# Gates read back and multiplied block by block ahead of the second expert product, in place of all of them during the first

## The chip, the core and the metric

The kernel runs on one core of a Trainium2 chip. The core has five engines with a queue each, and each runs its queue strictly in order: PE (TensorE, matrix products, with its weight loads shown as PEld), DVE (VectorE), ACT (ScalarE), POOL (GpSimd) and SP (SyncE, which here only issues DMAs). The metric is device microseconds of one execution, as the median of several runs.

## What is computed

The reference is one block of a gated delta-rule layer followed by one block with sparse attention and a mixture of single-neuron experts. The change touches only the experts. For 256 tokens `xc`, 16 experts are picked for each of 8 heads out of 16384:

```python
gate = jax.nn.softmax(best, axis=-1)
u_sel = u[expert]
v_sel = v[expert]
act = jax.nn.gelu(jnp.einsum('td,thkd->thk', xc, u_sel), approximate=False)
return jnp.einsum('thk,thkd->td', (gate * act), v_sel)
```

The kernel gathers nothing. It computes all 16384 activations `gelu(xc @ u.T)`, multiplies them with a gate that is zero for every expert that was not picked, and multiplies the result with all of `v`.

## The kernel before

**Tiling.** The 16384 experts are 128 blocks of 128. `G` is a tile of 128 partitions (experts of a block) by 128 blocks by 256 tokens in SBUF. The first expert product (`wstat` over `w_u`) fills it: each block takes 2 granules of weights (128 x 1024 values, 512 KB), 48 matmuls of 256 columns, and a Gelu on ACT for every two blocks. The second expert product (`w_v`, the loop `for half in range(2)`) runs over the blocks again, twice, once for each half of the 2048 output columns; block i takes one granule and 12 matmuls of 512 columns, 6 for each half of the tokens.

**Splits.** Each float32 operand is split into a high and a low part, and a product is three matmuls (high x high, high x low, low x high). `Stream` does this for the weights: SP loads a granule (`wraw`), ACT copies it to `wh`, DVE subtracts to get `wl`. There are three buffers of each, so that a granule can be split when PE has released the one three before. `split_h(i)` does the same for block i of `G` (ACT, then DVE; tiles `eog`, `eghl`, `eoj`, `ewg` in turn), two blocks ahead of PE.

**Gates.** `route()` picks the experts of each head, `gates_of(h)` computes gates and addresses (DVE), and 256 indirect DMAs of POOL scatter them into two arrays in HBM, `W_d[t]` for the two halves of 128 tokens, which are zeroed earlier. When the last scatter is issued, `gating()` starts: it reads `W_d` back in 64 loads of 256 KB (4 blocks, 128 tokens each; POOL's queue; three buffers, tags `og2`, `ghl` and `wt`), and for each load DVE multiplies the 4 blocks of `G` in place (128 x 512 elements). All 64 pairs are written before `drain()` returns, that is, before the second product begins. The tags `og2` and `ghl` are also those of two of the four kinds of `split_h` tiles.

**Other work of POOL and DVE in the second product.** `residual()` loads 8 pieces of the residual and 16 rows of layer-norm parameters (256 KB each, POOL's queue) and multiplies and adds them in `res_chunk` (16 instructions of DVE on 128 x 512 elements).

**What sets the order.** The program is written out by a Python model: generators in `sides` are pumped after each few matmuls, and `clk` holds a modelled time of PE, ACT, DVE and POOL, to which each instruction adds a price (`Paced`). `after(us)`, `on(engines)` and `spare(engine, us)` let a generator wait for these clocks. The model fixes only the order of each queue; on the chip, semaphores decide. As every instruction but the weight DMAs passes through one helper, all have line 129 in the profile, and are told apart by their tiles.

Of the kernel before, what the change touches and what calls it, by code (L numbers as in the profile page):

```python
# [10 lines left out]
F32 = mybir.dt.float32  # L11
F32R = mybir.dt.float32r
BF16 = mybir.dt.bfloat16
U32 = mybir.dt.uint32
# [3 lines left out]
OP = mybir.AluOpType  # L18
# [20 lines left out]
class Stream:  # L39
# [63 lines left out]
    def next(self, ahead=True):  # L103
        if ahead:
            self.ahead()
        while self.ns <= self.ng:
            self._split()
        p = self.parts.pop(self.ng)
        self.ng += 1
        return p  # L110
# [23 lines left out]
def _free(ap):  # L134
    return int(np.prod(ap.shape[1:]))
# [24 lines left out]
def tile_blocks(ctx, tc, P, out, dbg=None, stop=None):  # L160
    nc = tc.nc
    clk = {e: 0.0 for e in "PAVG"}
# [1 line left out]
    act = Paced(nc.scalar, "A", clk, _act_price())  # L164
    dve = Paced(nc.vector, "V", clk, lambda op, kw: 0.16 + 1.04e-3 * max(
        _free(kw[n]) for n in ("out", "in_", "in_values") if n in kw))
    pool = Paced(nc.gpsimd, "G", clk, lambda op, kw: 1.0 if op == "dma_start" else 2.4 if op == "indirect_dma_start" else 0.33 + 3.2e-3 * _free(kw["out"]))
    dbg = dbg or {}

    def ident_act(out, in_, scale=1.0, bias=0.0):  # L170
# [2 lines left out]
    def copy_act(out, in_):  # L173
        act.activation(out=out, in_=in_, func=AF.Copy)

    def tt(out, a, b, op):
        dve.tensor_tensor(out=out, in0=a, in1=b, op=op)
# [25 lines left out]
    def _take(side):  # L203
        s = free.pop(0)
        t = psp.tile([128, 512], F32, name=f"bank{s}")
        held[id(t)] = (s, side, t)
        side_held[0] += side
        return t
# [14 lines left out]
    def bank():  # L223

        n = 0
        while not free:
            pump()
            n += 1
            assert n < 1000
        return _take(0)  # L230

    granules, start = [], {}
    for nm in ("w_kv", "w_dn", "w_out", "w_in2", "w_out2", "w_q", "w_u", "w_v"):
        if nm in P:
            a = P[nm]
# [30 lines left out]
    def pump(n=1):  # L266
        for _ in range(n):
            if clk["P"] == mark[0]:
                clk["P"] += 0.4
            mark[0] = clk["P"]  # L270
            for g in list(sides):
                try:
                    next(g)
                except StopIteration:
                    sides.remove(g)

    def after(us):

        t = clk["P"] + us
        while clk["P"] < t:  # L280
            yield

    def on(engines="", lat=0.3):

        t = max([clk["P"]] + [clk[e] for e in engines]) + lat
        while clk["P"] < t:
            yield

    def spare(e, us):

        while clk[e] > clk["P"] + us:
            yield
# [16 lines left out]

    def wstat(n, xh, xl, nk, done, side=1, pre=None):  # L310

        for c0 in range(0, n, 2):
            m = min(2, n - c0)
            pt = bank()
            for c in range(m):
                for g in range(nk // 8):
                    wh, wl = (t.rearrange("p (k e) -> p k e", e=128) for t in ws.next())
                    for k in range(8):
                        kk = g * 8 + k
                        if pre is not None and c0 + c == 0:  # L320
# [864 lines left out]
    W_d = [dram.tile([128, 128, 128], F32, name=f"W_d{t}") for t in range(2)]  # L1185
# [359 lines left out]
    G = gp.tile([128, 128, T], F32, name="G")  # L1545
    rs_ = ExitStack()
    ctx.callback(rs_.close)
    rp = rs_.enter_context(tc.tile_pool(name="rp", bufs=1, side="right"))
    ghl = rp.tile([128, 2, T], F32R, name="ghl")
    for tag, n in (("og2", 1), ("oj", 2), ("wg", 2)):  # L1550
        for _ in range(n):
            rp.tile([128, (2 if n == 1 else 1) * T], F32R, name="e" + tag, tag=tag, bufs=n)
    rp.tile([128, 24], F32, name="gap")
    small = rp.tile([128, 64], F32, name="small")
    wt0 = rp.tile([128, 2, 2, 128], F32, name="wt")
    put_at = wt0[:, 0].rearrange("p a t -> p (a t)").rearrange("p (t k) -> p t k", t=2).bitcast(U32)
    put_val = wt0[:, 1].rearrange("p a t -> p (a t)").rearrange("p (t k) -> p t k", t=2)

    def carve(b0, shape, dt=F32):

# [29 lines left out]
    pool.iota(tok, pattern=[[0, 1]], base=0, channel_multiplier=1, allow_small_or_imprecise_dtypes=True)  # L1590
    sk = carve(83, [2, 128])
    act.dma_start(out=sk, in_=P["sk"])
    st4 = {"q": 0, "ib": 0, "put": 0}

    def q_done(c0, m, pt):
        copy_act(qp[:, c0:c0 + 2, :], pt.rearrange("p (c t) -> p c t", c=2))
# [12 lines left out]
    def route():  # L1609
        for h in range(8):  # L1610
            while st4["q"] <= h:
                yield
            ps = yield from get()
            for t in range(2):
                for f in range(2):
                    pe.matmul(out=ps[:, (2 * t + f) * 128:(2 * t + f) * 128 + 128],
                              lhsT=qp[:, 2 * h + f, t * 128:t * 128 + 128], rhs=sk[:, f, :], start=True, stop=True)
            yield
            s = ssb[h % 2]
            copy_act(s, ps.rearrange("p (t f k) -> p t f k", t=2, f=2))  # L1620
            put(ps)
            yield from on("A")
            for t in range(2):
                for f in range(2):
                    top16(vals[:, t, h, f, :], idxs[:, t, h, f, :], s[:, t, f, :], wrk[:, :128])
                    yield from spare("V", SV)
                tt(cand, bc(vals[:, t, h, 0, :, None], [128, 16, 16]), bc(vals[:, t, h, 1, None, :], [128, 16, 16]), OP.add)
                top16(best[:, t, h, :], pos[:, t, h, :], cand.rearrange("p a b -> p (a b)"), wrk)
                yield from spare("V", SV)
            yield from gates_of(h)  # L1630
        sides.append(gating())
# [39 lines left out]
    def gating():  # L1671

        wts = []

        def load(n):
            b, t = 4 * (n // 2), n % 2
            wt = rp.tile([128, 4, 128], F32, name="wt", tag=WT[n % 3])
            pool.dma_start(out=wt, in_=W_d[t][:, b:b + 4, :])
            wts.append(wt)

        yield from on("G", 4)
        for n in range(2):
            load(n)
        yield from after(4)
        for n in range(64):
            b, t = 4 * (n // 2), n % 2
            if n + 2 < 64:
                load(n + 2)
            while st4["ib"] < b + 4:
                yield  # L1690
            g = G[:, b:b + 4, t * 128:t * 128 + 128]
            tt(g, g, wts[n], OP.mult)
            yield from after(1.0)
            yield from spare("V", 1.5)
        split_h(0)
        split_h(1)

    WT = ("og2", "ghl", "wt")
    HS = {}
    EH = (("og2", 1), ("ghl", 1), ("oj", 2), ("wg", 2))  # L1700

    def split_h(i):

        i = i % 128
        tag, n = EH[i % 4]
        if n == 1:
            e = rp.tile([128, 2, T], F32R, name="e" + tag, tag=tag)
            a, b = e[:, 0, :], e[:, 1, :]
        else:
            a, b = (rp.tile([128, T], F32R, name="e" + tag, tag=tag, bufs=2) for _ in range(2))  # L1710
        copy_act(a, G[:, i, :])
        dve.follow("A")
        tt(b, G[:, i, :], a.bitcast(F32), OP.subtract)
        HS[i] = (a, b)
# [8 lines left out]
        drain()  # L1723
        return
    wstat(128, hh, hl, KT, u_done)
    drain()
    hs.close()


    vp = ctx.enter_context(tc.tile_pool(name="vp", bufs=1))  # L1730
    hres = vp.tile([128, 2, D], F32, name="hres")
    row = [vp.tile([128, D], F32, name=f"row{n}") for n in range(2)]
    bst2 = small[:, :48].rearrange("p (m c s) -> p m c s", m=2, c=4)
    mv2 = small[:, 48:52].rearrange("p (m s) -> p m s", m=2)
    rs2, wk2, nm2 = (small[:, n:n + 2].rearrange("p (m s) -> p m s", s=1) for n in (52, 54, 56))
    dg = rp.tile([128, 2, 128], F32, name="dg", tag="wt")
    st5 = {"res": False}
    RES = 4

# [62 lines left out]
    for half in range(2):  # L1802
# [14 lines left out]
        if half == 0:  # L1817
            while not st5["res"]:
                pump()
            for m in range(2):  # L1820
                for n in range(2):
                    sides.append(later(v_sum_g, n, m, acc[m][n]))
    drain()
    fin = [[bank() for _ in range(2)] for _ in range(2)]
    for m in range(2):
        for n in range(2):
# [145 lines left out]
```

## Time and profile before

| | us |
|---|---|
| median of 3 runs | 2832.1 |
| the runs | 2824.86 to 2833.19 |
| the profiled execution | 2828.32 |
| its span, first to last instruction | 2826.6 |
| PE busy | 2743.3 (97%) |
| DVE busy | 1829.9 (65%) |
| ACT busy | 1401.8 (50%) |
| POOL busy | 630.3 (22%) |

Times within the trace count from the start of the span. The first expert product ends at 2079.5 us, the second begins at 2106.5 us, its second half at about 2454 us. The granted clock of PE is given as a share of full speed (2.4 GHz).

### The profile page before, as it was taken

Reading aid. Unit: us, or ns where it says so; the run is one execution under the profiler, and the core shown is the slowest. Engines: PE = TensorE matmul, PEld = TensorE weight load, DVE = VectorE, ACT = ScalarE, POOL = GpSimd, SP = SyncE. Lnnn points to the kernel's source line nnn. Section 1 sums busy time; section 2 is a strip of 40 time slices with the busy share of each in tenths; the row PEclk is TensorE's granted clock in tenths of the full one; section 3 lists DMA queues with packets and bytes.
Section 4 is the critical chain, followed back from the end, with each engine's and each line's share of the span. In section 5 each row is a group of like instructions: output and inputs, shape, how many; then the busy total and the mean of one; then the engine's idle time right before and its main releaser. Section 6 shows DMA issues by size and latency. Waiting matters only on the chain.

```text
span 2826.6 us, 49454 instructions
## 1 busy us (share of the span) xinstructions
PE 2743.3 (97%) x19193; PEld 2520.4 (89%) x19193; DVE 1829.9 (65%) x3447; ACT 1401.8 (50%) x1955; POOL 630.3 (22%) x917
## 2 busy tenths in 40 slices
PE   9999999999999999999999999999759999999998
PEld 7999999999788999889999999999748888888886
DVE  5747777775654746657999995444556655665555
ACT  7456666665543545444544454444225455555553
POOL 0001546654001000000444444455330000000000
PEclk9999999999999999999999999999889999999999
DMA  8536655555588885456665666666786766666664
GB/s 302 184 121 188 202 162 179 168 171 160 192 247 239 255 256 179 150 164 197 181 193 180 187 194 197 195 194 195 238 279 205 221 194 194 191 196 194 194 194 134
DMA packets 170363, 555.83 MB, mean 197 GB/s; under 512 B 29088, under 2 KB 30680, under 8 KB 169616
## 3 DMA queue, kind: packets, MB, share of 16 engines
q1 hardware_dynamic: 144720, 507.05, 57.7%
q0 software_dynamic: 21584, 36.36, 4.8%
q10 hardware_dynamic: 3824, 9.26, 0.9%
q8 instruction: 150, 2.46, 0.4%
q14 instruction: 85, 0.70, 0.1%
HBM read 529.61 MB, written 22.90 MB: 195 GB/s over the span
## 4 chain that ended last, share of the span: by engine, by line
PE 89%; DMA 5%; DVE 4%; issue 1%; ACT 1%; POOL 0%; ACTq 0%; SPq 0%; DVEq 0%; POOLq 0%
PE bank L129 89%; DMA wt<-W_d 2%; DVE wl L129 1%; DVE G L129 1%; DMA W_d<-wt 1%; DMA wrawwraw<-in_w_kv 0%; DMA wrawwraw<-in_w_out 0%; DVE hres L129 0%; ACT wh L129 0%; DMA wrawwraw<-in_w_v 0%; DVE small L129 0%; ACT y L129 0%; DMA hot<-in_bucket_hot 0%; DMA hres<-n_d 0%; DVE sso L129 0%
## 5 line engine op out<-in xcount | busy, mean ns | idle before, releaser
L129 DVE TENSOR_TENSOR wl<-wrawwraw,wh 128x1024 fp32r<-128x1024 f32 (+1 forms) x837 | 1021.8, 1224 | 748.0 <-ACT wh L129 746.8
L129 ACT ACTIVATE wh<-wrawwraw 128x1024 fp32r<-128x1024 f32 (+1 forms) x837 | 885.9, 1059 | 1106.3 <-PE bank L129 889.1
L129 PE MATMUL bank<-hh,wl 128*128 128x256 f32 x3376 | 940.6, 279 | 22.6 <-DVE wl L129 22.6
L129 PE MATMUL bank<-hh,wh 128*128 128x256 f32 x3376 | 947.1, 281 | 1.1 <-ACT hh L129 1.1
L129 PE MATMUL bank<-hl,wh 128*128 128x256 f32 x3376 | 939.3, 278 | 0.1
L129 PEld LDWEIGHTS bank<-hh,wl 128*128 128x128 f32 x3376 | 637.2, 189 | 25.7 <-DVE wl L129 25.5
L129 PEld LDWEIGHTS bank<-hh,wh 128*128 128x128 f32 x3376 | 637.5, 189 | 2.6 <-ACT hh L129 1.5
L129 PEld LDWEIGHTS bank<-hl,wh 128*128 128x128 f32 x3376 | 637.9, 189 | 0.8 <-DVE hl L129 0.5
L129 POOL DMA_INDIRECT W_d<-wt x256 | 313.6, 1225 | 392.8 <-DVE G L129 177.2
L129 PE MATMUL bank<-wh,eog 128*128 128x512 f32 x512 | 148.3, 391 | 27.0 <-ACT eog L129 27.0
L129 DVE TENSOR_TENSOR wlx<-wrawx,whx 128x1024 fp32r<-128x1024 f32 x96 | 118.0, 1230 | 82.2 <-ACT whx L129 82.1
L129 ACT ACTIVATE whx<-wrawx 128x1024 fp32r<-128x1024 f32 x96 | 101.8, 1060 | 120.8 <-PE bank L129 106.8
L129 PE MATMUL bank<-wh,ewg 128*128 128x512 f32 x512 | 147.4, 389 | 0.0
L129 PE MATMUL bank<-wh,eoj 128*128 128x512 f32 x512 | 147.4, 389 | 0.0
L129 PE MATMUL bank<-wh,eghl 128*128 128x512 f32 x512 | 147.4, 389 | 0.0
L129 PEld LDWEIGHTS bank<-wh,eog 128*128 128x128 f32 x512 | 96.7, 189 | 47.2 <-ACT eog L129 27.2
L129 POOL TENSOR_TENSOR hres<-hres,row 128x512 f32<-128x512 f32 x4 | 5.8, 1476 | 575.6 <-DVE hres L129 575.6
L129 PEld LDWEIGHTS bank<-wh,eoj 128*128 128x128 f32 x512 | 96.1, 188 | 20.0
L129 PEld LDWEIGHTS bank<-wh,eghl 128*128 128x128 f32 x512 | 96.2, 188 | 19.9
L129 PEld LDWEIGHTS bank<-wh,ewg 128*128 128x128 f32 x512 | 96.1, 188 | 20.0
L129 PE MATMUL bank<-gh,wh 128*128 128x256 f32 x392 | 110.6, 282 | 0.0
L129 PE MATMUL bank<-gl,wh 128*128 128x256 f32 x392 | 108.4, 277 | 0.0
(381 smaller groups left out, 4448.7 us busy)
## 6 DMA issues: line engine op xcount, KB each, us to landing
wrawwraw<-in_w_u SPq DMA_DIRECT2D x256, 512.0 KB, 4.2
wrawwraw<-in_w_v SPq DMA_DIRECT2D x256, 512.0 KB, 4.3
wrawwraw<-in_w_dn SPq DMA_DIRECT2D x134, 512.0 KB, 4.2
wrawwraw<-in_w_out SPq DMA_DIRECT2D x73, 512.0 KB, 3.9
wrawwraw<-in_w_in SPq DMA_DIRECT2D x61, 512.0 KB, 4.6
wrawx<-in_w_dn SPq DMA_DIRECT2D x44, 512.0 KB, 3.7
W_d<-y SPq DMA_DIRECT2D x64, 256.0 KB, 5.5
wrawwraw<-in_w_q SPq DMA_DIRECT2D x32, 512.0 KB, 3.8
```

The costliest lines, as they stand in the source:

```text
L129: return f(*a, **kw)
```

## The change

- `gating()` now goes block by block. A load is two DMAs of 64 KB (128 partitions x 128 tokens each) for the two halves of the tokens, into one of three buffers of a tag `wt` of its own; the two tiles `put_at` and `put_val` from which the scatters are made hold two of these three until the scatters are done. The loads of blocks 0 to 2 are issued first, and that of block b + 3 behind the multiplication of block b.
- DVE multiplies one block (128 x 256 elements) at a time, 128 instructions in place of 64, at a pace of one in 1.8 us of the modelled PE time.
- The first product no longer waits for `gating()` to end; `split_h(i)` waits, in the model's order, until block i is multiplied (`st4["mul"]`).
- The model's price of an indirect DMA goes from 2.4 to 2.55 us.
- `small` shrinks, `bst2` moves to the pool `vp`, and `dg` is allocated later, which changes no instruction.

```diff
-    pool = Paced(... 2.4 if op == "indirect_dma_start" else ...)
+    pool = Paced(... 2.55 if op == "indirect_dma_start" else ...)
...
-    wt0 = rp.tile([128, 2, 2, 128], F32, name="wt")
-    put_at = wt0[:, 0].rearrange("p a t -> p (a t)").rearrange("p (t k) -> p t k", t=2).bitcast(U32)
-    put_val = wt0[:, 1].rearrange("p a t -> p (a t)").rearrange("p (t k) -> p t k", t=2)
+    put_at = rp.tile([128, 2, 128], U32, name="put_at", tag="wt", bufs=3)
+    put_val = rp.tile([128, 2, 128], F32, name="put_val", tag="wt", bufs=3)
...
-        def load(n):
-            b, t = 4 * (n // 2), n % 2
-            wt = rp.tile([128, 4, 128], F32, name="wt", tag=WT[n % 3])
-            pool.dma_start(out=wt, in_=W_d[t][:, b:b + 4, :])
+        def load(b):
+            wt = rp.tile([128, 2, 128], F32, name="wt", tag="wt", bufs=3)
+            for t in range(2):
+                pool.dma_start(out=wt[:, t], in_=W_d[t][:, b, :])
             wts.append(wt)
 
         yield from on("G", 4)
-        for n in range(2):
-            load(n)
+        for b in range(3):
+            load(b)
         yield from after(4)
-        for n in range(64):
-            b, t = 4 * (n // 2), n % 2
-            if n + 2 < 64:
-                load(n + 2)
-            while st4["ib"] < b + 4:
+        t0 = clk["P"]
+        for b in range(128):
+            while st4["ib"] <= b or clk["P"] < t0 + 1.8 * b:
                 yield
-            g = G[:, b:b + 4, t * 128:t * 128 + 128]
-            tt(g, g, wts[n], OP.mult)
-            yield from after(1.0)
-            yield from spare("V", 1.5)
-        split_h(0)
-        split_h(1)
+            yield from spare("V", 2)
+            g = G[:, b, :].rearrange("p (h t) -> p h t", h=2)
+            tt(g, g, wts[b], OP.mult)
+            st4["mul"] = b + 1
+            if b + 3 < 128:
+                load(b + 3)
...
+        while st4["mul"] <= i:
+            pump()
         copy_act(a, G[:, i, :])
...
     wstat(128, hh, hl, KT, u_done)
-    drain()
+    while st4["ib"] < 128:
+        pump()
+    split_h(0)
+    split_h(1)
```

Three places show what moves. DVE's queue late in the first product; `wl` is the split of a weight granule, `G<-G,wt` a multiplication with gates. Before:

```order
L129 TENSOR_TENSOR wl_23035<-wrawwraw_22967,wh_23034 128x1024
L129 TENSOR_TENSOR wl_23065<-wrawwraw_22998,wh_23064 128x1024
L129 TENSOR_TENSOR G<-G,wt 128x4x128 x2
L129 TENSOR_TENSOR wl_23102<-wrawwraw_23032,wh_23101 128x1024
L129 TENSOR_TENSOR G<-G,wt 128x4x128 x2
L129 TENSOR_TENSOR wl_23139<-wrawwraw_23062,wh_23138 128x1024
L129 TENSOR_TENSOR G<-G,wt 128x4x128 x2
```

The same queue now:

```order
L129 TENSOR_TENSOR wl_23459<-wrawwraw_23395,wh_23458 128x1024
L129 TENSOR_TENSOR wl_23499<-wrawwraw_23425,wh_23498 128x1024
L129 TENSOR_TENSOR G<-G,wt 128x256
L129 TENSOR_TENSOR wl_23533<-wrawwraw_23456,wh_23532 128x1024
L129 TENSOR_TENSOR G<-G,wt 128x256
L129 TENSOR_TENSOR wl_23567<-wrawwraw_23496,wh_23566 128x1024
L129 TENSOR_TENSOR G<-G,wt 128x256
```

The first multiplication stands 14 weight splits later: 24 splits stood between it and the first `split_h` before, and 10 now. Before, all 64 multiplications stood ahead of that `split_h`; now 16 of 128 do.

DVE's queue in the second product, where `residual()` has its first chunk (`hres` with `row`; the `e` tiles are `split_h`). Before:

```order
L129 TENSOR_TENSOR wl_24563<-wrawwraw_24516,wh_24562 128x1024
L129 TENSOR_TENSOR hres<-hres,row_24024 128x512
L129 TENSOR_TENSOR hres<-hres,row_24025 128x512
L129 TENSOR_TENSOR hres<-hres,row_24024 128x512
L129 TENSOR_TENSOR hres<-hres,row_24025 128x512
L129 TENSOR_TENSOR ewg<-G,ewg 128x256
L129 TENSOR_TENSOR wl_24590<-wrawwraw_24538,wh_24589 128x1024
```

Now:

```order
L129 TENSOR_TENSOR G<-G,wt 128x256 x2
L129 TENSOR_TENSOR eoj<-G,eoj 128x256
L129 TENSOR_TENSOR wl_24585<-wrawwraw_24526,wh_24584 128x1024
L129 TENSOR_TENSOR G<-G,wt 128x256
L129 TENSOR_TENSOR hres<-hres,row_23906 128x512
L129 TENSOR_TENSOR hres<-hres,row_23907 128x512
L129 TENSOR_TENSOR hres<-hres,row_23906 128x512
L129 TENSOR_TENSOR hres<-hres,row_23907 128x512
L129 TENSOR_TENSOR ewg<-G,ewg 128x256
L129 TENSOR_TENSOR wl_24615<-wrawwraw_24552,wh_24614 128x1024
```

One or two multiplications (37 in 25 weight splits) now stand between the splits of the second product, and the residual's instructions come among them. From the first `split_h` to the last multiplication there are 78 weight splits, 80 of `G`, 112 multiplications and the 16 of the residual.

POOL's queue. Before, the residual's loads stand behind all 64 loads of the gates:

```order
L129 DMA wt<-W_d_9527 128x512
L129 DMA wt<-W_d_9528 128x512
L129 DMA hres<-n_d 128x512 x2
L129 DMA row_24024<-in_ln1rows 128x512
L129 DMA row_24025<-in_ln1rows 128x512
```

Now they are dealt out among 256 smaller ones, one after four to ten of these:

```order
L129 DMA wt<-W_d_9527 128x128
L129 DMA wt<-W_d_9528 128x128
L129 DMA hres<-n_d 128x512
L129 DMA wt<-W_d_9527 128x128
L129 DMA wt<-W_d_9528 128x128
L129 DMA wt<-W_d_9527 128x128
L129 DMA wt<-W_d_9528 128x128
L129 DMA wt<-W_d_9527 128x128
L129 DMA wt<-W_d_9528 128x128
L129 DMA hres<-n_d 128x512
```

Each load waits for DVE's multiplication of the block three before, and so do the residual's loads queued behind it.

## Rows read from the trace of the kernel before

**Rows 1.** The page, in 40 slices of the span.

```profile
PE   9999999999999999999999999999759999999998
```

**Rows 2.** Windows: length, then busy us (instructions) of PE, PEld, DVE, ACT, POOL; clock, DMA, GB/s.

```profile
1300.00:1980.00 680.00, 678.27 (x5933) 677.67 (x5932) 502.63 (x1349) 313.83 (x338) 306.54 (x250) 1.00 0.63 190
1980.00:2106.00 126.00, 78.60 (x624) 75.86 (x622) 72.02 (x90) 30.97 (x33) 45.18 (x79) 0.84 0.76 250
2106.00:2454.00 348.00, 347.22 (x1524) 287.06 (x1525) 208.47 (x273) 175.34 (x259) 9.04 (x17) 1.00 0.68 207
```

**Rows 3.** Waits from 1980 to 2110 us: who for whom, us, times, longest.

```profile
DVE G L129 <- DMA wt<-W_d: 51.1, 39, 13.1
...
PE bank L129 <- ACT eog L129: 27.0, 1, 27.0
...
PE bank L129 <- DVE wl L129: 20.9, 11, 10.6
```

**Rows 4.** DVE in order of time about its first multiplication: start, length, instruction, idle before.

```profile
1983.68 1.23 DVE L129 TENSOR_TENSOR wl<-wrawwraw,wh 128x1024 fp32r<-128x1024 f32 x1 [1.50 <-ACT wh L129]
1998.02 0.69 DVE L129 TENSOR_TENSOR G<-G,wt 128x512 f32<-128x512 f32 x1 [13.11 <-DMA wt<-W_d]
```

**Rows 5.** The chain that ended last, its pieces about one load: start, length, what.

```profile
2068.12 0.28 issue
2068.41 4.15 DMA wt<-W_d
2072.58 0.70 DVE G L129
```

**Rows 6.** ACT and PE in order of time between the two products.

```profile
2079.49 0.60 ACT L129 ACTIVATE G<-bank 128x512 f32<-128x512 f32 x1 [1.31 <-PE bank L129]
2106.01 0.42 ACT L129 ACTIVATE eog<-G 128x256 fp32r<-128x256 f32 x1 [25.92 <-DMA hres<-n_d]
...
2106.48 1.22 PE L129 MATMUL bank<-wh,eog 128*128 128x512 f32 x2 [27.02 <-ACT eog L129]
...
2110.65 0.62 PE L129 MATMUL bank<-wh,eghl 128*128 128x512 f32 x2
```

**Rows 7.** PE and DVE in order of time, three granules of the second product.

```profile
2301.69 0.62 PE L129 MATMUL bank<-wh,ewg 128*128 128x512 f32 x2
...
2307.13 0.62 PE L129 MATMUL bank<-wh,eghl 128*128 128x512 f32 x2
...
2302.99 1.23 DVE L129 TENSOR_TENSOR wl<-wrawwraw,wh 128x1024 fp32r<-128x1024 f32 x1 [1.16 <-ACT wh L129]
```

**Rows 8.** POOL in order of time at the first loads of the gates.

```profile
1993.90 0.97 POOL L129 DMA_INDIRECT W_d<-wt  x1 [0.30 <-issue]
...
1996.32 1.09 POOL L129 DMA_DIRECT2D wt<-W_d  x2 [0.69 <-DMA W_d<-wt]
```

**Rows 9.** Tile `wt` from 2000 to 2080 us: DMA from issue to landing.

```profile
DMA to landing us min/median/max: 2.9/3.9/5.7
```

**Rows 10.** Groups from 2110 to 2470 us: shape, count, busy us, mean ns, idle before.

```profile
L129 DVE TENSOR_TENSOR wl<-wrawwraw,wh 128x1024 fp32r<-128x1024 f32 x132 | 161.7, 1225 | 141.2 <-ACT wh L129 141.2
...
L129 DVE TENSOR_TENSOR eog<-G,eog 128x256 fp32r<-128x256 f32 x33 | 13.8, 419 | 0.0
...
L129 DVE TENSOR_TENSOR hres<-hres,row 128x512 f32<-128x512 f32 x18 | 12.1, 689 | 0.3
```

**Rows 11.** DMA from 2083 to 2100 us: POOL's queue, its loads.

```profile
q0 software_dynamic: 920, 3.03, 62.8%
...
wt<-W_d POOLq DMA_DIRECT2D x12, 256.0 KB, 3.1
```

**Rows 12.** DMA from 1700 to 1960 us: POOL's queue, its scatters.

```profile
q0 software_dynamic: 3040, 0.05, 0.8%
...
W_d<-wt POOLq DMA_INDIRECT x95, 4.5
```

**Rows 13.** DMA from 2200 to 2400 us: SP's queue, the weights of the second product.

```profile
q1 hardware_dynamic: 10597, 38.56, 61.5%
```

More of the change, by code (lines that the diff above doesn't have):

```diff
@@ L166, in tile_blocks @@
         _free(kw[n]) for n in ("out", "in_", "in_values") if n in kw))
-    pool = Paced(nc.gpsimd, "G", clk, lambda op, kw: 1.0 if op == "dma_start" else 2.4 if op == "indirect_dma_start" else 0.33 + 3.2e-3 * _free(kw["out"]))
+    pool = Paced(nc.gpsimd, "G", clk, lambda op, kw: 1.0 if op == "dma_start" else 2.55 if op == "indirect_dma_start" else 0.33 + 3.2e-3 * _free(kw["out"]))
     dbg = dbg or {}
@@ L1552, in tile_blocks @@
             rp.tile([128, (2 if n == 1 else 1) * T], F32R, name="e" + tag, tag=tag, bufs=n)
-    rp.tile([128, 24], F32, name="gap")
-    small = rp.tile([128, 64], F32, name="small")
-    wt0 = rp.tile([128, 2, 2, 128], F32, name="wt")
-    put_at = wt0[:, 0].rearrange("p a t -> p (a t)").rearrange("p (t k) -> p t k", t=2).bitcast(U32)
-    put_val = wt0[:, 1].rearrange("p a t -> p (a t)").rearrange("p (t k) -> p t k", t=2)
+    rp.tile([128, 8], F32, name="gap")
+    small = rp.tile([128, 16], F32, name="small")
+    put_at = rp.tile([128, 2, 128], U32, name="put_at", tag="wt", bufs=3)
+    put_val = rp.tile([128, 2, 128], F32, name="put_val", tag="wt", bufs=3)
     def carve(b0, shape, dt=F32):
@@ L1592, in tile_blocks @@
     act.dma_start(out=sk, in_=P["sk"])
-    st4 = {"q": 0, "ib": 0, "put": 0}
+    st4 = {"q": 0, "ib": 0, "mul": 0}
     def q_done(c0, m, pt):
@@ L1673, in gating @@
         wts = []
-        def load(n):
-            b, t = 4 * (n // 2), n % 2
-            wt = rp.tile([128, 4, 128], F32, name="wt", tag=WT[n % 3])
-            pool.dma_start(out=wt, in_=W_d[t][:, b:b + 4, :])
+        def load(b):
+            wt = rp.tile([128, 2, 128], F32, name="wt", tag="wt", bufs=3)
+            for t in range(2):
+                pool.dma_start(out=wt[:, t], in_=W_d[t][:, b, :])
             wts.append(wt)
         yield from on("G", 4)
-        for n in range(2):
-            load(n)
+        for b in range(3):
+            load(b)
         yield from after(4)
-        for n in range(64):
-            b, t = 4 * (n // 2), n % 2
-            if n + 2 < 64:
-                load(n + 2)
-            while st4["ib"] < b + 4:
-                yield
-            g = G[:, b:b + 4, t * 128:t * 128 + 128]
-            tt(g, g, wts[n], OP.mult)
-            yield from after(1.0)
-            yield from spare("V", 1.5)
-        split_h(0)
-        split_h(1)
-    WT = ("og2", "ghl", "wt")
+        t0 = clk["P"]
+        for b in range(128):
+            while st4["ib"] <= b or clk["P"] < t0 + 1.8 * b:
+                yield
+            yield from spare("V", 2)
[4 more added lines that the diff above has]
+                load(b + 3)
     HS = {}
@@ L1732, in tile_blocks @@
     row = [vp.tile([128, D], F32, name=f"row{n}") for n in range(2)]
[L1733 to L1736, printed above, removed]
+    bst2 = vp.tile([128, 2, 4, 6], F32, name="bst2")
+    mv2 = small[:, :4].rearrange("p (m s) -> p m s", m=2)
+    rs2, wk2, nm2 = (small[:, n:n + 2].rearrange("p (m s) -> p m s", s=1) for n in (4, 6, 8))
     st5 = {"res": False}
@@ L1823, in tile_blocks @@
     drain()
+    dg = rp.tile([128, 2, 128], F32, name="dg", tag="wt", bufs=3)
     fin = [[bank() for _ in range(2)] for _ in range(2)]
```

## The prediction

> **What bounds the kernel now.** I read the page first: PE is at nine tenths or more in all but a few of the 40 slices, and the one hole in its middle is two slices of seven and five tenths [rows 1]. PE sets the time, so the question is what makes that hole. The windows give its size. From 1300 to 1980 us PE is busy throughout at a granted clock of 1.00, and 5933 matmuls are recorded in 680 us, 8.73 a microsecond. From 1980 to 2106 it is busy for 78.6 of 126 us, with 624 matmuls, at a mean clock of 0.84. Behind that it is full again, 347.2 of 348 us [rows 2].
>
> The waits say who held it: PE waited 20.9 us for splits of weights by DVE and 27.0 us for ACT's first split of G, and DVE waited 51.1 us for the gates to come back from HBM [rows 3]. DVE's queue shows the first of these: its split at 1983.68 us ended at 1984.91, and then it stood 13.1 us before its first multiplication, since the last scatter was issued at 1993.9 us and the loads behind it at 1995 to 1997 [rows 4, 8]. The weight splits queued behind that multiplication were late, and PE with them. The chain then shows a loop of one load (4.15 us there), one multiplication (0.70) and 0.28 us until the next load is issued [rows 5]; with three buffers, three loads are in flight at a time. There are 64 loads, and the last of them is used only 26 us after the first product has ended: the last Gelu begins at 2079.49, the first split of G at 2106.01, the first matmul of the second product at 2106.48 [rows 6]. The profile puts that last wait down to a load of `hres`; as the multiplications end at that very moment, I take it for them.
>
> **What the change removes.** Both waits have one cause, gates read too late for a product that has nothing else to do. In DVE's queue the first multiplication now stands 14 weight splits later. A granule takes PE 2.72 us, half of the 5.44 us from 2301.69 to 2307.13 [rows 7]. So DVE comes to it 38.1 us later, at about 1984.9 + 38.1 = 2023 us. The gates are there at 1998 [rows 4], so the wait of 13.1 us goes, with 25 us to spare. In front of the second product stand 16 multiplications instead of 64, spread over 10 granules (27 us, in which they need 16 x 0.42 = 6.7 us of DVE), and none of the other 112 is waited for there.
>
> The 624 matmuls recorded in the hole need 624 / 8.73 = 71.5 us at the full rate. The first product then ends at 1980 + 71.5 = 2051.5 us. What is late next is the hand-over itself: the last Gelu (0.60 us from its start), then ACT's split of block 0, from whose start to PE's first matmul it is 0.47 us [rows 6]. That is 1.1 us, and the second product begins at 2052.6 instead of 2106.5: 53.9 us less. Its first granule took 4.17 us (2106.48 to 2110.65) instead of 2.72, since PE had stood still for 27 us and came back at a lower clock; with a gap of 1 us I expect it at full clock, 1.4 us more. Together **55.3 us**.
>
> **What the change adds, on DVE.** 128 multiplications of 256 columns in place of 64 of 512. The trace has no gate multiplication of 256 columns; the split of G is the same operation on the same shape, 419 ns [rows 10]. From the first split of G to the last multiplication there are 78 weight splits (1.225 us), 80 of G, 112 multiplications and 16 instructions of the residual (0.689) [rows 10]: 95.6 + 33.5 + 46.9 + 11.0 = 187 us, in 78 x 2.72 = 212 us. DVE is 88% full there and still not the bound. In the 25 granules in which the residual has its chunks it is: 25 splits, 26 of G, 37 multiplications and 16 of the residual are 30.6 + 10.9 + 15.5 + 11.0 = 68.0 us, and 25 granules take 68.0 us. There it has nothing to spare. A split is ready 2.9 us before PE wants it (it ends at 2304.22, three granules behind the one whose buffer it took, which PE comes to at 2307.13) [rows 7], but the densest place (one multiplication, four of the residual, a split of G, a weight split: 4.82 us in a granule of 2.72) takes 2.1 us of this. So in these 68 us whatever DVE waits for its gates is lost by PE, nearly all of it.
>
> **What it adds, in waits for the gates.** The load of block b + 3 is issued behind the multiplication of block b. From one to the next of the same buffer it takes 0.42 us of DVE, 0.28 to the issue [rows 5], 0.54 for the first DMA of the pair (two took 1.09 on POOL [rows 8]) and the landing L of the second: 1.24 + L. The queue gives it three multiplications' time: 3 x 68.0 / 37 = 5.5 us in the dense stretch, 3 x 88 x 2.72 / 128 = 5.6 over all. So DVE waits when L is above 4.3 us. The trace has no load of 64 KB in 512-byte rows. The nearest rows are those of 256 KB, beside the same weights: 2.9, 3.9 in the median, and 5.7 at most [rows 9]. With the median nothing waits. In the dense stretch the transfers are more: weights 0.524 MB in 2.72 us are 193 GB/s, gates 37 x 0.131 MB in 68 us are 71, and 16 loads of the residual, which now stand in the same queue, 62: 326 GB/s, where 250 was the mean in the hole [rows 2]. For this stretch I take L half way between 3.9 and 5.7, 4.8 us: 0.5 us for each of 37 / 3 loops, 6 us. The ends are 0 (L = 3.9) and 1.43 x 12.3 = 18 us (L = 5.7). A gain cannot come from here, as PE has 0.8 us of idle time in this stretch before [rows 2].
>
> The rest costs nothing: on POOL, 256 DMAs of 0.54 us are 138 us in the 240 us over which they spread; the residual's loads no longer run ahead, but their chunks are due only by the end of the half; the model's new price of a scatter changes only where the multiplications stand, which is counted.
>
> **Sum.** 2828.3 us (the profiled execution) - 55.3 + 6 = 2779.0. The median of the runs is 3.8 us above that execution, the fastest run 3.5 below; I add 1 and forecast **2780 us**.
>
> **Rival A: the loop of loads becomes the bound.** If L is 5.0 us over all 128 blocks, DVE waits 1.24 + 5.0 - 5.6 = 0.64 us in each of 43 loops, 27 us: 2828.3 - 55.3 + 27 = 2800. With 5.7 it is 1.34 x 43 = 58 us, and the gain is gone: 2831. For it: three buffers now hold 128 KB each, half of what they held, so the same latency moves fewer gates. Against it: what bounds it is latency against the pace, and the median, with four times as much in one load, is 3.9.
>
> **Rival B, slower than before: the DMA engines are full.** All loads share 16 engines with the weights. In the last 17 us of the hole twelve loads of 256 KB took 62.8% of the engines [rows 11]: 17 x 0.628 / 12 = 0.89 us of all 16 for each, of 128 pieces of 2 KB. Now there are 256 loads of 128 pieces of 512 bytes. If the price goes by bytes, a load takes a quarter, 0.22 us; if it goes by pieces, 0.89. From 1996 us to the end of the half there are 55.5 + 348 = 404 us; the weights take 61.5% of these [rows 13], 248 us, the residual's 24 loads 24 x 0.89 = 21. With 0.22 the gates add 56 us, 325 of 404, and nothing overflows; with 0.89 they add 228, in all 497, 93 more than there is: 2828.3 - 55.3 + 93 = 2866. It makes the kernel slower from 0.74 us a load. Against it speak the scatters, also 128 pieces each (of 4 bytes): 95 of them took 0.8% of 260 us [rows 12], 0.022 us each, so the number of pieces alone is cheap. They are writes, though, and these are reads.
>
> The Trainium skill speaks for rival B ("DMA: Bandwidth & Descriptors", sections "Bandwidth" and "Rules for kernel authors"): it wants transfers coalesced, calls those under 64 KB mostly overhead, and lists 0.95 us for 64 KB. An estimate by that figure is 256 x 0.95 = 243 us of gates, 108 us more than there is, and 2881 us. The scatters' 0.022 us does not agree with it as a price of the engines' time; no row here has a load of 64 KB, so the rule is not refuted.
>
> **Rival C: it does not do what it says**, because the first multiplication waits again. It would need the gates 25 us later than in this trace; POOL's queue up to the last scatter is the same instructions, so I give it no chance of its own.
>
> **How the numbers follow.** The forecast, with L between 3.9 and 5.7 in the dense stretch alone and the spread of the runs, holds 2768 to 2793: 0.72. Rival A up to a part of the gain, 2793 to 2823: 0.15. Rival A with all of it given back, 2824 to 2840: 0.06. Rival B: 0.07. Below the forecast's lower end there is nothing to win. A measurement of this kernel tells about 0.3% (8.5 us) from no change: faster is below 2823.6, so 0.87; within it 0.06; slower 0.07. The range reaches from 2767 to 2806, which takes in the forecast and the lower half of rival A.
>
> **What would show it.** In the profile after: no hole at 1980 us, DVE's first multiplication at about 2023 us without a wait, the first product done near 2051 and the second begun near 2053 at a clock of 1.00; multiplications of about 0.42 us; POOL's loads landing in 3 to 4 us, near 5 among the residual's; PE waiting for `wl` for some 6 us in the first half, and there only in the residual's stretch; DMA busy for near 0.85 in it. Rival A would show waits of DVE for `wt` in most loops; rival B would show DMA above 0.95 from 2000 us on, and weight loads landing far later than now. I would be wrong if the second product began near 2053 and its first half still took far more than 348 + 18 us.

## The result and the profile after

| | before | after |
|---|---|---|
| median, us | 2832.4 | 2796.1 |
| the runs (four each) | 2824.9 to 2833.2 | 2790.5 to 2800.4 |
| ratio | | 0.988 [0.985, 0.990] |
| profiled execution | 2828.3 | 2790.5 |
| its span | 2826.6 | 2788.7 |
| second product begins | 2106.5 | 2050.5 |
| its first half lasts, us | 355.4 | 375.1 |

The kernel is faster by 36 us, 16 less than forecast. The last two lines say why. The half is counted from the first matmul of the second product to the first `SCALAR_TENSOR_TENSOR` on `hres`, which ends it. The second product begins 56.0 us earlier, and its first half is 19.7 us longer; the difference, 36.3, is all but 1.5 us of the 37.8 us between the two profiled executions. Of all the kernels reported below, one run lies far off and stays out of its kernel's ratio: 7098.2 us with the price of a scatter back at 2.4.

First what came as forecast. The page's row of PE, 40 slices of the span (compare [rows 1]): the hole in the middle has gone, and two slices of nine and eight tenths stand where the first half of the second product runs.

```profile
PE   9999999999999999999999999999999899999998
```

DVE in order of time about its first multiplication (start, length, instruction; compare [rows 4]). It has no wait.

```profile
2020.62 1.22 DVE L129 TENSOR_TENSOR wl<-wrawwraw,wh 128x1024 fp32r<-128x1024 f32 x1 [1.49 <-ACT wh L129]
2021.77 0.42 DVE L129 TENSOR_TENSOR G<-G,wt 128x256 f32<-128x256 f32 x1
```

The hand-over between the products, ACT and PE in order of time (compare [rows 6]): PE stands 0.99 us instead of 27. In its first granule it stands another 0.72 us, for DVE's part of the split of `G`.

```profile
2049.56 0.60 ACT L129 ACTIVATE G<-bank 128x512 f32<-128x512 f32 x1 [1.77 <-PE bank L129]
...
2050.06 0.41 ACT L129 ACTIVATE eog<-G 128x256 fp32r<-128x256 f32 x1
...
2050.52 0.73 PE L129 MATMUL bank<-wh,eog 128*128 128x512 f32 x2 [0.99 <-ACT eog L129]
...
2052.44 1.19 PE L129 MATMUL bank<-wh,eog 128*128 128x512 f32 x4 [0.72 <-DVE eog L129]
...
2054.39 0.62 PE L129 MATMUL bank<-wh,eghl 128*128 128x512 f32 x2
```

Now what did not. The windows of [rows 2], and the stretch in which PE loses (length, then busy us and instructions of PE, PEld, DVE, ACT, POOL; clock, DMA, GB/s):

```profile
1980.00:2106.00 126.00, 124.29 (x854) 114.38 (x853) 77.76 (x111) 59.59 (x77) 59.66 (x103) 1.00 0.79 245
2106.00:2454.00 348.00, 334.59 (x1446) 272.14 (x1445) 233.38 (x355) 164.52 (x241) 96.83 (x183) 0.99 0.73 229
...
2110.00:2240.00 130.00, 116.69 (x486) 92.10 (x485) 91.14 (x155) 53.60 (x81) 71.94 (x136) 0.97 0.80 254
```

A granule of 12 matmuls takes 2.72 us [rows 7], so the last stretch has room for 574. It holds 486: 88 x 0.227 = 20 us are lost there, which is all that the half is longer by. The residual's chunks lie in this stretch, from 2123 to 2204 us; 61 of the 88 matmuls are lost among them, and 20 in the 36 us behind them. DVE is busy for 91 of the 130 us, so it is not its work alone.

The waits from 1980 to 2440 us (who for whom: us, times, longest; compare [rows 3]):

```profile
ACT wh L129 <- DMA wrawwraw<-in_w_v: 88.3, 49, 6.3
DVE G L129 <- DMA wt<-W_d: 57.9, 50, 4.7
PEld bank L129 <- DVE wl L129: 19.3, 14, 3.4
PE bank L129 <- DVE wl L129: 13.3, 12, 2.9
```

DVE's wait for gates in the 130 us alone (2110 to 2240 us):

```profile
DVE G L129 <- DMA wt<-W_d: 34.3, 23, 4.7
```

DVE waits 57.9 us for gates, as much as before (51.1), but 50 times, most often one or two microseconds; 34.3 us of it lie in the 130 us in which PE loses. PE waits 12 times for splits of weights, 13.3 us, and its weight loads (PEld) 14 times, 19.3 us, much of it at the same time. After its two longest stops, 2.64 and 2.94 us, its granted clock is 0.50 of full speed (1.2 GHz) for some 3 us each; this is the second of them:

```profile
2222.99 1.22 PE L129 MATMUL bank<-wl,eog 128*128 128x512 f32 x2 [2.94 <-DVE wl L129]
```

```profile
2223.00:2226.00 3.00, 3.00 (x7) 2.42 (x8) 3.00 (x7) 0.00 (x0) 2.03 (x5) 0.50 0.85 257
```

ACT waits 88.3 us for weights. SP, which issues their loads, itself waits for DVE to be done with a buffer, 7.3 us at most, and a load can be slow besides: the chain of waits holds one of weights that took 7.97 us.

```profile
2122.38 7.97 DMA wrawwraw<-in_w_v
```

The landing of the gates, tile `wt` from 2040 to 2280 us (compare [rows 9]):

```profile
DMA to landing us min/median/max: 2.0/4.0/7.1
```

A load of 64 KB lands no earlier than one of 256 KB did from 2000 to 2080 us before (3.9 in the median). In the same queue and stretch now, though, the residual's loads of 256 KB take 5.5 us: side by side, the smaller ones were quicker. One loop of the loads is seen in order of time in DVE's and POOL's queues:

```profile
2136.85 0.42 DVE L129 TENSOR_TENSOR G<-G,wt 128x256 f32<-128x256 f32 x1
2137.57 1.06 POOL L129 DMA_DIRECT2D wt<-W_d  x2 [0.24 <-DVE G L129]
...
2138.35 0.43 DVE L129 TENSOR_TENSOR G<-G,wt 128x256 f32<-128x256 f32 x1 [1.07 <-DMA wt<-W_d]
...
2140.17 0.42 DVE L129 TENSOR_TENSOR G<-G,wt 128x256 f32<-128x256 f32 x1
...
2143.14 0.43 DVE L129 TENSOR_TENSOR G<-G,wt 128x256 f32<-128x256 f32 x1 [2.56 <-DMA wt<-W_d]
2143.49 0.42 DVE L129 TENSOR_TENSOR eog<-G,eog 128x256 fp32r<-128x256 f32 x1
2143.82 1.22 DVE L129 TENSOR_TENSOR wl<-wrawwraw,wh 128x1024 fp32r<-128x1024 f32 x1
...
2145.09 0.73 PE L129 MATMUL bank<-wl,eog 128*128 128x512 f32 x2 [1.74 <-DVE wl L129]
```

The multiplication at 2136.85 frees a buffer; POOL issues its pair at once, and the pair has landed at 2143.1. The third multiplication behind it stands in DVE's queue at 2140.58 and waits 2.56 us for that load. Behind it stand the split of `G` and the weight split, and PE waits 1.74 us for the latter. The loop took 6.29 us: nearly the 1.24 of the prediction and the landing, 4.95, which the chain of waits gives (start, length, what):

```profile
2138.10 4.95 DMA wt<-W_d
```

### The profile page after: what moved, and what is told of

The parts are those of the page before. It is cut to its first block, busy times and chain, and to the rows that moved or that the text cites. A ratio compares the mean times of both kernels' runs of the same rounds, so it can differ in the third digit from the quotient of the medians.

```text
span 2788.7 us, 49891 instructions
## 1 busy us (share of the span) xinstructions
PE 2739.4 (98%) x19193; PEld 2514.4 (90%) x19193; DVE 1832.7 (66%) x3511; ACT 1402.0 (50%) x1955; POOL 726.6 (26%) x1109
## 4 chain that ended last, share of the span: by engine, by line
PE 87%; DMA 5%; DVE 5%; issue 1%; ACT 1%; POOL 1%; ACTq 0%; POOLq 0%; DVEq 0%; SPq 0%
PE bank L129 87%; DMA wt<-W_d 3%; DVE wl L129 2%; DVE G L129 1%; DMA wrawwraw<-in_w_v 1%; POOL wt L129 1%; DMA wrawwraw<-in_w_kv 0%; DMA wrawwraw<-in_w_out 0%; ACT wh L129 0%; DVE hres L129 0%; DMA wrawwraw<-in_w_u 0%; ACT y L129 0%; DMA hot<-in_bucket_hot 0%; DVE bst L129 0%; DVE small L129 0%
## 5 line engine op out<-in xcount | busy, mean ns | idle before, releaser
L129 POOL DMA_INDIRECT W_d<-put_val,put_at x256 | 309.3, 1208 | 395.1 <-DVE G L129 179.5
L129 POOL DMA_DIRECT2D wt<-W_d x256 | 135.6, 535 | 139.2 <-DVE G L129 129.4
```

Source lines behind the costliest of these rows:

```text
L129: return f(*a, **kw)
```

## The experiments

Three theories stood against each other for the 20 us. **Theory 1**: the loop of three loads, latency against pace, makes DVE wait, and where DVE has no time to spare PE pays. **Theory 2**: it is DVE's own work, the multiplications among the splits and the residual. **Theory 3**: the DMA engines, shared between gates and weights, make both late. Three of the kernels below leave out a part of the computation, and each of these was run once. The time that tells most is that of the first half of the second product (375.1 us; 355.4 before).

**No loads beyond the first three blocks** (Theory 2 against the others).

```diff
-            tt(g, g, wts[b], OP.mult)
+            tt(g, g, wts[b % 3], OP.mult)
...
-            if b + 3 < 128:
-                load(b + 3)
```

> The changed kernel without the read-back of the gates behind the first three blocks (all 128 multiplications stay where they are and use the three tiles that were loaded), so DVE has the same work and the gates take no transfers and no waits. The second product's first half, from its first matmul to the first sum of an output bank, took 355.4 us before and 375.1 us with the change, 19.7 us more. Theory 1 (DVE waits in the loop of three buffers: load, multiplication, next load): the 19.7 us go, about 356 us. Theory 2 (DVE has too much to do in the residual's stretch, whatever the loads do): at least 12 of the 19.7 us stay, 367 us or more. Theory 3 (the transfers crowd out the weights): about 356 us.

Measured: 2764.3 us, and the half takes 355.7 us. All multiplications are there, and nothing is lost against the half of before. Theory 2 falls as the sole cause; Theories 1 and 3 both forecast this.

**The multiplication cut to two columns**, with the loads as they are. The second new line keeps the model's clock, and with it the order of the queues.

```diff
-            tt(g, g, wts[b], OP.mult)
+            tt(g[:, :, :1], g[:, :, :1], wts[b][:, :, :1], OP.mult)
+            clk["V"] += 0.264
```

> The changed kernel with multiplications of 2 elements a partition in place of 256, in the same places of the same queues; the loads and the waits stay, and DVE is relieved of some 0.3 us in each of 128 blocks. Theory 1 (loop of loads): the loop shrinks from about 1.24 us + landing by 0.3 us, so most of the loss stays: 365 us or more for the first half. Theory 2 (DVE too full): DVE falls to some 85% in the residual's stretch, and the first half takes 355 to 359 us. Theory 3 (transfers): 370 us or more, since the transfers are the same.

Measured: 2785.8 us, the half 370.5. A multiplication takes 161 ns instead of 421, 29 us of DVE less in the 112 of the second product, and 4.6 of the 19.7 us go. DVE's waits for the gates grow from 58 to 68 us, nearly all of it in front of these 112. This speaks against Theory 2; Theories 1 and 3 both allow it.

```profile
L129 DVE TENSOR_TENSOR G<-G,wt 128x2 f32<-128x2 f32 x112 | 17.2, 161 | 64.3 <-DMA wt<-W_d 63.6
```

**No chunks of the residual on DVE** (its loads stay): the body of `res_chunk` is left out.

> The changed kernel without the residual's 16 multiplications and additions on DVE (11 us of work left out); its loads stay. If DVE loses PE's time by the sum of its work and its waits for gates, the stretch in which it was 100% full falls to 84%, waits of up to 0.4 us a granule find room, and 8 to 12 of the 19.7 us go: first half 363 to 367 us. If the waits alone cost it, 372 us or more; if the work alone did, 356.

Measured: 2780.6 us, the half 366.8: 8.3 us of the 19.7 go. DVE waits 60.7 us, about as long as with the chunks, but PE's waits for splits fall from 13.3 to 6.0 us. In the stretch that lost 88 matmuls PE now loses 43:

```profile
2110.00:2240.00 130.00, 124.66 (x531) 99.53 (x530) 88.31 (x151) 59.65 (x87) 78.50 (x148) 0.99 0.87 273
```

So some half of the price needs the chunks beside the waits. The waits are needed for all of it, since without the loads nothing was lost.

**Five buffers instead of three**, at the same pace. Their room comes from one of the four kinds of split tiles of `G`.

```diff
-            wt = rp.tile([128, 2, 128], F32, name="wt", tag="wt", bufs=3)
+            wt = rp.tile([128, 2, 128], F32, name="wt", tag="wt", bufs=5)
...
-        for b in range(3):
+        for b in range(5):
             load(b)
...
-            if b + 3 < 128:
-                load(b + 3)
+            if b + 5 < 128:
+                load(b + 5)
...
-    EH = (("og2", 1), ("ghl", 1), ("oj", 2), ("wg", 2))
+    EH = (("og2", 1), ("ghl", 1), ("oj", 2))
```

> The changed kernel at its own pace of 1.8 us with five buffers for the gates instead of three (the space comes from the splits of G, which get three tiles in turn instead of four); the loop then has 5 x 1.84 = 9.2 us for multiplication, issue and landing. Work of DVE and bytes moved in each microsecond are as in the changed kernel. Theory 1 (latency of the loop): no landing is late, the first half takes 355 to 359 us instead of 375, the kernel 2776 to 2782 us. Theory 3 (the transfers take the weights' share): 370 us or more, the kernel 2792 to 2800.

Measured: 2783.0 us, the half 357.8. The waits (1980 to 2440 us):

```profile
DVE G L129 <- DMA wt<-W_d: 7.8, 6, 3.0
PE bank L129 <- DVE wl L129: 2.4, 4, 0.7
```

The same bytes at the same pace: 50 waits become 6, and 17.3 of the 19.7 us go. Theory 1 holds. Theory 3 falls as far as late weights would cost this without the waits for gates. Why a landing of gates lasts as long as it does is not settled by this: the engines' load may have a part in it, and five buffers cover it. The median is only 13 us below the changed kernel's: two of the four runs took 2774 and 2775 us, the other two 2791 and 2793, and in the last of these, the profiled one, the first product ran slower, which is the last section's matter.

**A slower pace**, one multiplication in 2.6 us of the model's PE time instead of 1.8.

```diff
-            while st4["ib"] <= b or clk["P"] < t0 + 1.8 * b:
+            while st4["ib"] <= b or clk["P"] < t0 + 2.6 * b:
```

> The changed kernel with one multiplication in 2.6 us of the modelled time instead of 1.8 (one for each block of the product). The loop of three buffers has 7.8 us instead of 5.5, DVE's densest 27 us fall from 99% to 96%, the gates' transfers from 71 to 49 GB/s. Theory 1: landings under 6.5 us cost nothing, first half 356 to 360 us, the kernel 2778 to 2783 us. Theory 2: the bursts of the residual still cost a little, 358 to 363 us. Theory 3: as the sum of bytes in the half is the same, a third to a half of the loss stays, 362 to 368 us, the kernel near 2788.

Measured: 2770.8 us, ratio to before 0.982 [0.977, 0.987], better than expected. The half takes 353.5 us. The waits for the gates, and the window that lost 20 us:

```profile
DVE G L129 <- DMA wt<-W_d: 5.5, 6, 2.0
```

```profile
2110.00:2240.00 130.00, 130.00 (x575) 107.59 (x574) 100.88 (x161) 64.55 (x96) 60.84 (x116) 1.00 0.87 279
```

PE is busy throughout and does 575 matmuls instead of 486. DVE does more there (100.9 us against 91.1) and the DMA engines move more (279 GB/s against 254): neither was the limit. With the waits for gates the loss is gone.

**A pace of 2.2**, between the two.

> The pace of the multiplications is one in 2.2 us of the modelled PE time, between the 1.8 of the changed kernel and the 2.6 of the slower one. If the latency of the loop of three loads against the pace is what costs, the step is a threshold: three multiplications now give a load 6.6 us, and the loop takes 1.24 us and the landing, 4.0 us in the median, so only the few late landings (up to 7.1 us) still hold DVE: its waits for the gates fall from 58 us to under 15, the first half of the second product takes 355 to 361 us (375.1 changed, 353.5 at 2.6), and the time is 2770 to 2780 us. If it were bytes per microsecond, the loss falls with the rate alone, by a fifth: about 371 us and 2791.

Measured: 2779.7 us, 0.985 [0.981, 0.988]; the half 361.0, DVE's waits 29.9 us in 25. The half is at the edge of what was expected of a threshold, and the waits are twice as long: it is rather a slope. With three buffers a load has three multiplications' time: 5.4 us at 1.8, 6.6 at 2.2, 7.8 at 2.6. The loop takes 1.24 us and a landing of 4.0 in the median and 6.5 to 7.1 at most, 5.2 and 7.7 to 8.3. So, by this estimate, at 2.2 the later ones of the landings still hold DVE, and only at 2.6 hardly any.

**The residual (loads and chunks) behind the last multiplication**, at the old pace.

```diff
         yield from after(20)
+        while st4["mul"] < 128:
+            yield
         act.activation(out=wk2[:, 0, :] ...
```

> The changed kernel at its pace of 1.8 us, with the residual (loads and chunks) only after the last multiplication instead of among them. DVE is then 84% full while the gates come. Theory 1 with DVE's sum of work and waits: DVE waits as often, but finds room, first half 358 to 364 us, the kernel 2779 to 2786. If the loop alone were the bound (landing above the pace): 370 us or more, about 2794.

Measured: 2775.4 us, 0.982 [0.979, 0.985], the half 363.4. Here the waits and the density are apart:

```profile
DVE G L129 <- DMA wt<-W_d: 48.3, 49, 3.1
PE bank L129 <- DVE wl L129: 0.8, 3, 0.5
```

From 2110 to 2240 us alone:

```profile
DVE G L129 <- DMA wt<-W_d: 34.0, 31, 3.1
```

The windows:

```profile
2110.00:2250.00 140.00, 139.50 (x610) 113.78 (x610) 102.14 (x175) 68.87 (x101) 77.42 (x147) 1.00 0.83 258
2270.00:2290.00 20.00, 18.15 (x71) 13.74 (x70) 10.76 (x15) 9.45 (x14) 2.60 (x5) 0.91 0.92 323
```

DVE waits as long in the 130 us as in the changed kernel (34.0 and 34.3 us), and PE waits under 1 us for its splits: without the residual DVE has the time. From 2110 to 2250 us PE does 610 matmuls, 8 short of the full rate (2 us), instead of 88 short in 130 us. The kernel without chunks, whose residual's loads stay among those of the gates, lost 43 there; so these loads, which this run moves as well, seem to carry a part. No run moves them alone. Another 17 (4 us) are lost at 2270 to 2290 us, where the residual's loads, no longer held by the gates, start one behind another and the DMA engines are 92% busy.

**The residual behind the last multiplication, and a pace of 2.2.**

> The pace of 2.2, and in addition the residual starts only when the last block is multiplied, so that its 16 instructions do not meet the gates. If a loss needs both the waits and a DVE that has no time left, what the slower pace leaves goes too: the first half takes 353 to 357 us, PE waits under 1 us for splits of weights, 2766 to 2776 us in all. If the residual's loads and chunks, now 24 loads and 16 instructions in the last 100 us of the half, are late there, the half is longer than at 2.2 alone and PE waits near 2400 us.

Measured: 2776.1 us, 0.983 [0.980, 0.986]; the half takes 359.0 us, above what was expected. DVE waits 3.5 us for gates in all. The windows:

```profile
2290.00:2310.00 20.00, 20.00 (x90) 16.57 (x89) 14.07 (x24) 10.51 (x16) 12.25 (x24) 1.00 0.85 255
2310.00:2330.00 20.00, 18.85 (x80) 14.42 (x79) 8.77 (x12) 8.36 (x13) 4.60 (x9) 1.00 0.99 346
2330.00:2350.00 20.00, 19.51 (x86) 16.17 (x87) 13.25 (x18) 11.52 (x17) 0.00 (x0) 1.00 0.71 217
```

From 2070 to 2310 us every window of 20 us holds 90 matmuls, as the first one here. Then the residual's loads come all at once, the DMA engines are 99% busy, and DVE has 12 instructions in 20 us, since it waits for weights. That is rival B in small: where the engines were full, the weights were late. In the changed kernel they were 80% busy in the stretch in which PE loses.

**The price of a scatter back at 2.4**, the rest as changed.

```diff
-    2.55 if op == "indirect_dma_start"
+    2.4 if op == "indirect_dma_start"
```

> The changed kernel with the old price of an indirect DMA in the model, 2.4 us: the first multiplication stands 14 weight splits earlier, as in the kernel before. DVE should come to it near 1985 us, wait some 13 us for the last scatters and the first loads, and PE should lose 8 to 10 us near 1990, as in the windows of before. The kernel 2803 to 2807 us where the changed one takes 2796. If the wait were hidden by the splits that stand ahead, 2796.

Measured: 2803.7 us, 0.991 [0.987, 0.994]. DVE in order of time:

```profile
1982.25 1.23 DVE L129 TENSOR_TENSOR wl<-wrawwraw,wh 128x1024 fp32r<-128x1024 f32 x1 [1.50 <-ACT wh L129]
2002.73 0.42 DVE L129 TENSOR_TENSOR G<-G,wt 128x256 f32<-128x256 f32 x1 [19.25 <-DMA wt<-W_d]
```

The first multiplication stands 14 granules earlier again and waits 19.25 us, and the second product begins at 2068.1 instead of 2050.5. So of the 56 us by which the start moved, 17.6 hang on a number of the model; a loss of 8 to 10 was expected. The half took 370.7 us, 4.4 less than in the changed kernel; the two profiled executions differ by the rest, 13.2 us, and the medians by 8. The intervals of the two ratios overlap, so a loss of time is not shown by them; the later start is.

**One array and one load for both halves of the tokens**, to set one load of 128 KB against two of 64.

```diff
-    W_d = [dram.tile([128, 128, 128], F32, name=f"W_d{t}") for t in range(2)]
+    W_d = dram.tile([128, 128, 2, 128], F32, name="W_d")
...
-            for t in range(2):
-                pool.dma_start(out=wt[:, t], in_=W_d[t][:, b, :])
+            pool.dma_start(out=wt, in_=W_d[:, b, :, :])
```

> The changed kernel with the two gate arrays laid side by side, so that one block comes in one DMA of 128 KB in 1 KB rows instead of two of 64 KB in 512-byte rows: 128 loads in place of 256, same bytes. Theory 1: the second issue (0.54 us) leaves the loop, so of the 19.7 us 8 to 12 stay, first half 363 to 367 us, the kernel 2784 to 2789. Theory 2: nothing changes for DVE, 373 to 376 us, the kernel 2796. Theory 3 with a price by pieces (half as many): more than half of the loss goes, under 365 us; with a price by bytes: no change.

Measured: 3134.7 us, ratio 1.108, and nothing on the question. All 256 scatters now go to one array, and POOL waits before 182 of them for an earlier one. POOL's waits, here and (the second line) in the changed kernel:

```profile
POOL W_d L129 <- DMA W_d<-put_val,put_at: 479.1, 182, 5.9
```

```profile
POOL W_d L129 <- DMA W_d<-put_val,put_at: 156.3, 95, 3.6
```

The scatters end at 2383 us, after the first product, and PE stands still meanwhile. Whether one load per block would land sooner stays open.

**The pace of 2.6 again**, beside the last two.

> The kernel at a pace of 2.6 once more, on the same chip as the two others, to set the three beside each other and to settle its interval: 2765 to 2773 us (2770.8 the first time, with one run at 2790.5). If the cost were only a matter of the loop, it is not faster than the two at 2.2 by more than 5 us.

Measured: 2772.1 us, 0.981 [0.978, 0.983], with a half of 353.5 us again. By the ratios it is some 20 us faster than the changed kernel (0.981 against 0.988), and 4 to 8 us faster than the two at 2.2, less than the runs of one kernel differ by, so these three are not told apart.

## Why the prediction was right, and where 16 us went

- **The waits that go: right.** The first multiplication was forecast at 2023 us without a wait and came at 2021.8; the first product done at 2051 and the second begun at 2052.6, and it began at 2050.5. Of the 2.1 us between, 0.8 are the rate: I had taken it from 1300 to 1980 us as 8.73 matmuls a microsecond, and an undisturbed stretch has 8.83 (2870 in 325 us, last section), by which the 624 matmuls take 70.7 instead of 71.5 us. The first granule ran at a granted clock of 1.00, as forecast, but took 3.87 us (2050.52 to 2054.39) instead of 2.72, since it waited for DVE: of the 1.4 us forecast there, 0.3 came.
- **DVE's work: right.** A gate multiplication took 421 ns (419 forecast). Without the waits the dense stretch does fit beside PE: 575 matmuls in 130 us at the slower pace, and 355.7 us for the half without loads, at the old pace.
- **The wait for gates: the term that was mis-sized**, 6 us with ends of 0 and 18; PE lost 14 us (61 matmuls) between the first and the last chunk, and 6 us just ahead of and behind them, where I had put nothing: 20 us, above the upper end. The loop's formula was right (6.29 us for a landing of 4.95). What failed is that I set one landing against a mean pace. I took 4.8 us for the residual's stretch; the median was 4.1 from 2110 to 2240 us, less than I took, and still DVE waited 34.3 us there, 19.9 of it among the chunks, and not 6. Landings spread from 2.0 to 7.1 us, and the multiplications do not stand evenly, two of them now next to each other and now 2 us apart. A late landing costs a wait, and an early one gives nothing back, as the next multiplication stands in a queue. So I read it that 50 waits came where the means (4.0 + 1.24 against 5.5) say none.
- **Who pays: nearly right.** I said that DVE has no spare time in the residual's stretch, so that its waits go to PE there, and not elsewhere. The runs show most of it: 34 us of waits from 2110 to 2240 us cost 20 there, and the same 34 us cost 2 with the residual moved away. But not all of a wait is lost where DVE is full, nor does the loss end with the chunks: 20 of the 88 matmuls are lost behind 2204 us. I left out that a late DVE also frees weight buffers late, so that SP issues weights late (ACT's 88.3 us; these waits alone cost little, since ACT waits 95.3 us with the residual moved away), and that PE's two longest stops halve its clock for some 3 us each, an estimated 3 us of the 20.
- **Rival A: its mechanism, less of its price.** Waits in most loops did come, 58 us of them, which it put at 2831. But 24 of the 58 lie outside the 130 us and cost next to nothing, and the other 34 cost 20. The time came out in the band that I had given to this rival at 0.15 (2793 to 2823), above the forecast's own band (2768 to 2793, 0.72). The stated range holds it because it took in the lower half of this rival; the start of the second product was foreseen, the size of the waits was not.
- **Rival B: refuted.** POOL's queue from 2040 to 2280 us (packets, MB, share of 16 engines) and its loads:

```profile
q0 software_dynamic: 9348, 21.51, 29.7%
...
wt<-W_d POOLq DMA_DIRECT2D x232, 64.0 KB, 4.0
hres<-n_d POOLq DMA_DIRECT2D x8, 256.0 KB, 5.5
```

29.7% of 240 us are 71 us; without the residual's 24 loads at 0.89 they are 50 us for 232 loads, 0.21 us each. The price is near that by bytes, as the lower bound had it. The estimate of 0.95 us by the Trainium skill ("DMA: Bandwidth & Descriptors", section "Bandwidth") does not hold as engine time here; the measurement decides. Its advice against small transfers (section "Rules for kernel authors") holds in another way: a load of a quarter of the size took 4.0 us to land where the residual's took 5.5, so a load moves far less in its time in flight.
- **The total.** 2828.3 - 56.0 + 19.7 - 1.5 elsewhere = 2790.5, the profiled execution; the median is 5.6 us above it, where I had added 1. So of the 16 us 11.5 are in the execution, and 4.6 are the place of the median among the runs.

## What to carry to other kernels

When loads are made smaller and issued behind the use of the buffer that they refill, do not count on their latency shrinking as they do (4.0 us for 64 KB here, 5.5 for 256 KB beside them): set buffers times pace against issue plus the **late** landings, not the median. What a wait costs depends on the time that the waiting engine has to spare, so ask what else was put in that stretch. Here a slower pace gave back all of the loss (375.1 to 353.5 us for the half), and moving the other work away 11.7 us of it. And an order that depends on a modelled price can move a good part of a start, as the scatter's 2.4 or 2.55 did with 17.6 of 56 us: check where it places the first use against the landing in the trace.

## What the runs showed of the hardware

**Matmuls 4% slower at a granted clock of 1.00.** The kernel at a pace of 2.6 was profiled twice, with spans of 2768.0 and 2785.1 us. Windows from 1725 to 2050 us of the first and then the second execution:

```profile
1725.00:2050.00 325.00, 325.00 (x2870) 325.00 (x2870) 150.38 (x131) 141.06 (x150) 149.74 (x128) 1.00 0.68 199
```

```profile
1725.00:2050.00 325.00, 325.00 (x2762) 325.00 (x2761) 142.27 (x121) 136.11 (x144) 159.86 (x119) 1.00 0.64 190
```

PE is busy throughout in both and waits for nothing, but does 108 matmuls fewer, 0.118 us each instead of 0.113. In the second execution this began at 1708.6 us, where one matmul took 0.39 instead of 0.28 us, and ended with the 1-us gap between the products at 2068 us; the second product then ran at the full rate (353.5 us for the half in both). 3.8% of 360 us are 14 of the 17 us; the other 3 lie ahead of 1250 us, where 26 matmuls fewer are recorded. The profile of the kernel with five buffers has the same stretch from about 1710 to 2066 us. What switches it is not known; as one kernel shows both, it is not the kernel alone.

**Scatters into one array went one by one** in this program. POOL's queue, with one array:

```profile
2200.72 0.97 POOL L129 DMA_INDIRECT W_d<-put_val,put_at  x1 [1.90 <-DMA W_d<-put_val,put_at]
2203.60 0.97 POOL L129 DMA_INDIRECT W_d<-put_val,put_at  x1 [1.91 <-DMA W_d<-put_val,put_at]
```

That is one in 2.9 us. With two arrays in turn POOL waits 156 instead of 479 us for them. Whether the chip or only the program's own semaphores ask for this wait is not shown.
